# Sixteen up-projection groups of a two-layer encoder trunk computed with seven products in place of eight

## The chip, the cores and the metric

The kernel runs on one NeuronCore of one Trainium2 chip. The metric is device microseconds of one execution. The five engines have a queue each and are named as the profile names them: PE (TensorE, matrix products; PEld are its weight loads), DVE (VectorE), ACT (ScalarE), POOL (GpSimd) and SP (SyncE, which here issues the loads). Engines wait for one another by semaphores. Matrix results are accumulated in PSUM, eight banks of 128 partitions x 512 fp32 numbers; everything else lives in SBUF.

## The reference: what is computed

256 tokens of width 2048 in fp32 go through two layers, and each layer ends in a gated feed-forward part. Only that part is touched here:

```python
def conv_ffn(x, w_up, conv_w, conv_b, w_down):
    u = x @ w_up                                  # 256 x 2048 by 2048 x 11264
    up = jnp.pad(u, ((0, 0), (1, 1), (0, 0)))
    u = c[0] * up[:, :-2] + c[1] * up[:, 1:-1] + c[2] * up[:, 2:] + conv_b
    gate, val = jnp.split(u, 2, axis=-1)          # 5632 each
    return (jax.nn.silu(gate) * val) @ w_down     # 5632 x 2048

x = x + conv_ffn(rms_norm(x, norm_ffn[layer]), w_up[layer], conv_w[layer], conv_b[layer], w_down[layer])
```

Layer 0 has pooling and attention ahead of it, layer 1 an mLSTM; both of these end in an output projection with a residual add.

## The kernel before, in words

All products are made in fp32r from two parts. A weight chunk w (128x1024 fp32) is split by ACT into a rounded high part (L89) and by DVE into the remainder, the low part (L90); both go into a tile hl. Activations have a high and a low part too (xx, L266 and L269). A product is then three matmuls: high x high, high x low, low x high.

`Stream` holds the list of all weight chunks in the order in which they are used. `next()` hands out the next split chunk and keeps loads five chunks and splits two chunks ahead in the order of the program; raw chunks rotate through six buffers (pool wraw), split ones through four (wsplit). So a cast of a new chunk waits until PE has finished the chunk that used the buffer, and a load until DVE has split the chunk in its buffer.

PE's order is the order of the program text (manual_schedule); DVE's, ACT's, SP's and POOL's queues are ordered by a scheduler, which at each moment takes what its own time line says is ready. Each queue is then worked off strictly in order. `Weave` (wv) places side tasks among the groups: a task is a generator that yields a delay in estimated microseconds.

A feed-forward layer (ffn_layer) has 44 tiles f of 128 gate and 128 value columns, in chunks of FCH = 4, 8, 8, 8, 8, 8 tiles. An up group (up, stat_group, L203) takes four weight chunks; for each of 16 K tiles PE makes two matmuls of 512 columns and two of 256, with the weights stationary and the tokens moving, into two PSUM banks pairs of the pool mm (two buffers). Then gather (ACT copy L366, DVE add L367) joins the parts, L890 multiplies by the norm's scale R, L894 to L897 do the convolution, L900 to L903 the gate and the split of the result into gt. After the up groups of chunk c come the four down groups of chunk c-1 (down): activations stationary, weights moving 512 columns at a time; L376 adds the result to the residual x.

The norm ahead of a layer (class Norm) is applied late. squares and block run after each quarter of the residual: ACT's sums of squares, PE transposes (xt, L254), the parts xx. finish then makes the scale: nsum (L282), rv_n (L208), POOL's power, four short DVE steps re_n (L212 to L215), the diagonal dg (L294), PE's product with ones (npr, L203) and its copy R (L299). PE executes npr inside the fourth weight chunk of the layer's first up group.

The PSUM pool ps (four single banks) serves transposes and small products.

Of the kernel before, what the change touches and what calls it, by code (L numbers as in the profile page):

```python
# [9 lines left out]
F32 = mybir.dt.float32  # L10
F32R = mybir.dt.float32r
AF = mybir.ActivationFunctionType
ALU = mybir.AluOpType
# [3 lines left out]
P = 128  # L17
D = 2048
S = 256
KT = D // P  # L20
# [11 lines left out]
FT = DFF // P  # L32
FCH = [4, 8, 8, 8, 8, 8]
CH = 8
# [7 lines left out]
NB = D // 512  # L42
# [22 lines left out]
class Stream:  # L65


    def __init__(self, nc, wpool, spool, srcs, load_ahead, split_ahead):
        self.nc, self.wpool, self.spool, self.srcs = nc, wpool, spool, srcs
        self.la, self.sa = load_ahead, split_ahead  # L70
        self.w, self.hl = {}, {}
        self.n_load = self.n_split = self.at = 0

    def load(self, pieces=1):
        i = self.n_load
        width = self.srcs[i].shape[-1]
        n = width // pieces
        w = self.wpool.tile([P, CH * P], F32, tag="w", name=f"w{i}")
        for c in range(0, width, n):
            self.nc.sync.dma_start(w[:, c : c + n], self.srcs[i][:, c : c + n])  # L80
        self.w[i] = w, n, width
        self.n_load += 1

    def split(self, then=None):
        i = self.n_split
        w, n, width = self.w.pop(i)
        hl = self.spool.tile([P, 2, CH * P], F32R, tag="hl", name=f"hl{i}")
        for c in range(0, width, n):
            (self.nc.vector.tensor_copy if i + c == 0 else self.nc.scalar.copy)(hl[:, 0, c : c + n], w[:, c : c + n])  # L89
            self.nc.vector.tensor_sub(hl[:, 1, c : c + n], w[:, c : c + n], hl[:, 0, c : c + n].bitcast(F32))  # L90
            then and then(c // n)
        self.hl[i] = hl
        self.n_split += 1
# [63 lines left out]
def trunk(ctx: ExitStack, tc: tile.TileContext, gx, xT, xn, call, catt, cml, weights, out):  # L157
    nc = tc.nc
# [7 lines left out]
    actp = pool("act", 1)  # L166
# [16 lines left out]
    first = ExitStack()  # L183
# [179 lines left out]
    def gather(tp, ps, name):  # L363

        tb = tp.tile([P, 2, S], F32, tag="tb", name=f"tb_{name}")
        a.copy(tb, ps[:, :, 1, :])  # L366
        v.tensor_add(tb, ps[:, :, 0, :], tb)  # L367
        return tb

    def bc(ap, n):  # L370
        return ap.unsqueeze(1).to_broadcast([ap.shape[0], n, ap.shape[1]])

    def residual(ps, b, eng=None):
        for t in range(2):
            xs = x[:, t, b * 512 : b * 512 + 512]
            v.tensor_add(xs, xs, ps[:, t])  # L376
# [495 lines left out]
    def ffn_layer(layer, norm, nxt):  # L872
        with ExitStack() as es:
            def lp(name, bufs):
                return es.enter_context(tc.tile_pool(name=name, bufs=bufs, reuse_waits="tile"))

            tp = lp(f"ff{layer}", 2)

            def cw(tl, j):
# [6 lines left out]
            def up(f, gt, i):  # L886
                ps = stat_group(xx, list(range(KT)), f"up{layer}_{f}")
                wv.until(lambda: norm.R is not None)
                u = gather(tp, ps, f"up{layer}_{f}")
                v.tensor_mul(u, u, bc(norm.R, 2))  # L890
# [8 lines left out]
                s_ = tp.tile([P, S], F32, tag="silu", name=f"s{layer}_{f}")  # L899
                a.activation(s_, y[:, 0, :], AF.Silu)  # L900
                v.tensor_mul(s_, s_, y[:, 1, :])
                a.copy(gt[:, i, 0, :], s_)
                v.tensor_sub(gt[:, i, 1, :], s_, gt[:, i, 0, :].bitcast(F32))  # L903

            def down_end(gt, b, kts):
# [27 lines left out]
            def down(c, gt, last):  # L933
                kts = list(range(FCH[c]))
                for b in range(NB):
                    if last and nxt is None and b == NB - 1:
                        down_end(gt, b, kts)
                        break
                    ps = mmp.tile([P, 2, 512], F32, tag="mm", name=f"dn{layer}_{c}_{b}")
                    mov_part(ps, lambda k: gt[:, k], kts, True, True)  # L940
                    residual(ps, b)
                    if last and nxt is None:
                        nc.sync.dma_start(out[:, :, b * 512 : b * 512 + 512], x[:, :, b * 512 : b * 512 + 512])
                    elif last:
                        nxt.add(b)

            wv.add(norm.finish(), 4.0)
            f, gts = 0, []
            for c, n in enumerate(FCH):
                gt = actp.tile([P, 8, 2, S], F32R, tag=f"B{c % 2}", name=f"g{layer}_{c}")  # L950
                gts.append(gt)
                for i in range(n):
                    up(f, gt, i)
                    f += 1
                if c:
                    down(c - 1, gts[c - 1], False)
            down(len(FCH) - 1, gts[-1], True)

    norms = [Norm(0), None]
    norms[1] = Norm(1)  # L960
# [64 lines left out]
    return np.concatenate(out)  # L1025


def _ffn_order():

    seq, u, d = [], 0, 0  # L1030
    for c, n in enumerate(FCH):
        seq += [("u", u + i) for i in range(4 * n)]
        u += 4 * n
        if c:
            m = FCH[c - 1] // 4 * 8
            seq += [("d", d + i) for i in range(m)]
            d += m
    m = FCH[-1] // 4 * 8
    seq += [("d", d + i) for i in range(m)]
    return seq  # L1040


# [98 lines left out]
```

## Time and profile before

| | us |
|---|---|
| time, three runs | 2205.48, 2205.55, 2205.71; median 2205.55 |
| profiled execution, span from first to last instruction | 2203.1 |
| PE busy | 2197.9 (100%) |
| DVE busy | 1525.5 (69%) |
| ACT busy | 1169.0 (53%) |
| matmuls of the 88 up groups | 984.2 |
| matmuls of the down groups | 471.3 |
| feed-forward layers, from the stages | 256 to 990 and 1468 to 2203 |

The table's busy times are from the page's first and fifth parts. The span is what the profiled execution has of its own; the runs' times also hold what lies around it, 2.45 us against the median. In rows of groups, the columns are line, engine, operation, output <- inputs, shapes and count, then busy time, the mean of one in nanoseconds, and the idle time of the engine just before them with what ended it. Rows of the timeline and of the chain start with the start time and the length.

### The profile page before, as it was taken

How to read it: one execution, taken by the hardware profiler on the slowest of the kernel's cores; microseconds unless marked ns; L12 is line 12 of the kernel's file. 1: busy time of each engine (PE TensorE's matmuls, PEld its weight loads, DVE VectorE, ACT ScalarE, POOL GpSimd, SP SyncE). 2: the span in 40 equal slices, each digit the busy share in tenths (PEclk: the TensorE clock that was granted, in tenths of full speed). 3: DMA queues.
4: the chain of work that ended last, by engine and by line, in shares of the span. 5: the costliest groups of instructions: out<-in, count | busy, mean ns of one | idle time of the engine just before them, and what ended most of it. 6: DMA issues, size and time to landing. Idle time of an engine off the chain costs nothing.

```text
span 2203.1 us, 30458 instructions
## 1 busy us (share of the span) xinstructions
PE 2197.9 (100%) x11616; PEld 1883.7 (86%) x11616; DVE 1525.5 (69%) x2172; ACT 1169.0 (53%) x1664; POOL 28.1 (1%) x40
## 2 busy tenths in 40 slices
PE   9999999999999999999999999999999999999999
PEld 8888888888888888889888888888888888888887
DVE  7686677776776767666767676667777677676764
ACT  7665555554554545456555454555555455454542
POOL 0020000000000000000000000000000000000000
PEclk9999999999999999999999999999999999999999
DMA  9555556556565666656565555556555656555664
GB/s 323 179 164 170 175 191 187 190 189 198 184 194 188 192 191 191 196 171 205 162 202 177 185 181 171 186 177 191 186 191 189 197 185 193 189 191 191 192 191 144
DMA packets 118036, 415.71 MB, mean 189 GB/s; under 512 B 13082, under 2 KB 15426, under 8 KB 117890
## 3 DMA queue, kind: packets, MB, share of 16 engines
q1 hardware_dynamic: 114656, 409.76, 58.2%
q10 hardware_dynamic: 3074, 3.75, 0.6%
q8 instruction: 91, 1.49, 0.3%
q14 instruction: 55, 0.45, 0.1%
q0 software_dynamic: 160, 0.26, 0.0%
HBM read 411.58 MB, written 2.14 MB: 188 GB/s over the span
## 4 chain that ended last, share of the span: by engine, by line
PE 100%; DVE 0%; issue 0%
PE up L203 45%; PE dn L203 21%; PE op L203 8%; PE mv L203 4%; PE mq L203 4%; PE mk L203 4%; PE mo L203 4%; PE qproj L203 3%; PE pool L203 1%; PE kproj L203 1%; PE vproj L203 1%; PE qk L203 1%; PE av L203 1%; PE end L203 0%; PE xt L254 0%; PE sc L203 0%
## 5 line engine op out<-in xcount | busy, mean ns | idle before, releaser
L90 DVE TENSOR_TENSOR hl<-w,hl 128x1024 fp32r<-128x1024 f32 (+2 forms) x772 | 939.1, 1218 | 466.6 <-ACT hl L89 464.8
L89 ACT CAST hl<-w 128x1024 fp32r<-128x1024 f32 (+1 forms) x771 | 806.9, 1047 | 677.3 <-PE dn L203 242.1
L203 PE MATMUL up<-xx,hl 128*128 128x512 f32 (+1 forms) x5632 | 984.2, 337 | 0.0
L203 PEld LDWEIGHTS up<-xx,hl 128*128 128x128 f32 x5632 | 857.9, 188 | 125.9
L203 PE MATMUL dn<-hl,g 128*128 128x512 f32 x2064 | 471.3, 389 | 0.0
L203 PEld LDWEIGHTS dn<-hl,g 128*128 128x128 f32 x2064 | 386.2, 188 | 79.5
L366 ACT COPY tb_up<-up 128x512 f32<-128x512 f32 x88 | 51.7, 587 | 154.0 <-PE up L203 154.0
L367 DVE TENSOR_TENSOR tb_up<-up,tb_up 128x512 f32<-128x512 f32 x88 | 60.8, 691 | 97.0 <-ACT tb_up L366 97.0
L894 ACT ACTIVATE y<-tb_up,cst 128x256 f32<-128x256 f32 x176 | 96.4, 595 | 47.0 <-DVE tb_up L890 47.0
L203 PE MATMUL mk<-xx,hl 128*128 128x512 f32 (+1 forms) x512 | 92.2, 337 | 0.0
L203 PE MATMUL mq<-xx,hl 128*128 128x512 f32 (+1 forms) x512 | 92.1, 337 | 0.0
L203 PE MATMUL mv<-hl,xx 128*128 128x512 f32 (+2 forms) x480 | 91.7, 350 | 0.0
L203 PE MATMUL op<-hl,cat 128*128 128x512 f32 x384 | 91.6, 393 | 0.0
L203 PE MATMUL mo<-hl,xx 128*128 128x512 f32 x384 | 90.4, 391 | 0.0
L203 PE MATMUL op<-hl,mcat 128*128 128x512 f32 x384 | 89.5, 392 | 0.0
L203 PEld LDWEIGHTS mq<-xx,hl 128*128 128x128 f32 x512 | 79.2, 188 | 11.6
L203 PEld LDWEIGHTS mk<-xx,hl 128*128 128x128 f32 x512 | 79.0, 188 | 11.4
L203 PEld LDWEIGHTS mv<-hl,xx 128*128 128x128 f32 x480 | 78.3, 189 | 11.2
L203 PEld LDWEIGHTS op<-hl,mcat 128*128 128x128 f32 x384 | 71.5, 188 | 14.6
L203 PEld LDWEIGHTS mo<-hl,xx 128*128 128x128 f32 x384 | 71.0, 188 | 14.2
L203 PEld LDWEIGHTS op<-hl,cat 128*128 128x128 f32 x384 | 70.9, 188 | 14.1
L895 DVE SCALAR_TENSOR_TENSOR y<-tb_up,cst,y 128x255 f32<-128x255 f32 x176 | 76.8, 478 | 0.0
(209 smaller groups left out, 1270.4 us busy)
## 6 DMA issues: line engine op xcount, KB each, us to landing
w<-in_up SPq DMA_DIRECT2D x352, 512.0 KB, 3.6
w<-in_dn SPq DMA_DIRECT2D x176, 512.0 KB, 4.1
w<-in_m_in SPq DMA_DIRECT2D x124, 512.0 KB, 4.1
w<-in_a_in SPq DMA_DIRECT2D x46, 512.0 KB, 4.4
w<-in_a_out SPq DMA_DIRECT2D x32, 512.0 KB, 3.4
w<-in_m_out SPq DMA_DIRECT2D x32, 512.0 KB, 3.5
w<-in_m_g SPq DMA_DIRECT2D x5, 432.0 KB, 3.4
x<-in_xn SPq DMA_DIRECT2D x4, 512.0 KB, 9.5
```

Of the source, the lines that this page charges most:

```text
L89: (self.nc.vector.tensor_copy if i + c == 0 else self.nc.scalar.copy)(hl[:, 0, c : c + n], w[:, c : c + n])
L90: self.nc.vector.tensor_sub(hl[:, 1, c : c + n], w[:, c : c + n], hl[:, 0, c : c + n].bitcast(F32))
L203: pe.matmul(out_, lhsT, rhs, start=start, stop=stop, skip_group_check=True)
L366: a.copy(tb, ps[:, :, 1, :])
L367: v.tensor_add(tb, ps[:, :, 0, :], tb)
L894: a.activation(y[:, j, :], u[:, j, :], AF.Identity, scale=cw(tl, 1), bias=cw(tl, 3))
L895: v.scalar_tensor_tensor(y[:, j, 1:S], u[:, j, 0 : S - 1], cw(tl, 0), y[:, j, 1:S], ALU.mult, ALU.add)
```

## The change

For four of the eight tiles of chunks 2 and 4, in both layers, the four up groups are replaced by one "unit" (quads). The 256 tokens are two row tiles, the K tiles are taken in eight pairs, and the weights of the four tiles form two halves of 512 columns: a 2x2 by 2x2 block product for each K pair. It is made with seven block products instead of eight, Winograd's form: four in phase one (banks p1, p5, p6, p4), three in phase two (p5 and p6 again, p1 again). The activations are now stationary, so the result has tokens in partitions: ACT and DVE drain the banks into c11, c12, c21, c22 with the norm's scale on the way, PE transposes them back (finish), and the convolution follows as before (tail).

The seven products need sums. Sums of weights are made by DVE in the raw chunk before the split: one 128x512 add for a "sum" chunk, two for a "chain" chunk. A unit has 16 chunks in phase one (eight sum, eight chain) and 12 in phase two (eight sum, four plain), 28 where 16 stood. Sums of activations (sums, eight per half: one add of 128x2048, five of 128x512, then four casts and four subtractions) go to sx once per layer, as a side task.

The product chunks are spread between other groups (_ffn_plan): a unit's chunks lie one by one between the chunks of the up and down groups of the two chunks ahead, and down groups are now placed between up groups instead of behind them. Loads run seven and splits three chunks ahead, with one more raw and one more split buffer in the feed-forward layers. The gate is computed in place in y. The product, its plan and the two places that the prediction speaks of:

```diff
     def split(self, then=None):
         i = self.n_split
-        w, n, width = self.w.pop(i)
-        hl = self.spool.tile([P, 2, CH * P], F32R, tag="hl", name=f"hl{i}")
+        w, n, width, kind = self.w.pop(i)
+        hl = self.home(i, False).tile([P, 2, CH * P], F32R, tag="hl", name=f"hl{i}")
+        l, r = w[:, 0:512], w[:, 512:1024]
+        if kind == "sum":
+            self.nc.vector.tensor_add(r, r, l)
+            self.sum = r
+        if kind == "chain":
+            self.nc.vector.tensor_add(l, l, self.sum)
+            self.nc.vector.tensor_add(r, r, l)
...
+            def sums():
+                vv = actp.tile([P, 2, KT // 2, S], F32, tag="B1", name=f"v{layer}")
+                for h in range(2):
+                    ks = slice(8 * h, 8 * h + 8)
+                    v.tensor_add(vv[:, 0], norm.xx[:, ks, 0, :].bitcast(F32), norm.xx[:, ks, 1, :].bitcast(F32))
+                    yield 5.0
...
+                    v.tensor_sub(s1, a21, a22)
+                    v.tensor_add(s3, a11, a21)
+                    yield 3.0
+                    v.scalar_tensor_tensor(s2, s1, -1.0, a11, ALU.mult, ALU.subtract)
+                    v.tensor_sub(s4, s3, a12)
+                    v.tensor_sub(s4, s4, a22)
+                    yield 4.0
+                    for j in range(4):
+                        hi, lo = (sx[:, j, 4 * h : 4 * h + 4, i, :] for i in range(2))
+                        a.copy(hi, raw[:, j])
+                        v.tensor_sub(lo, raw[:, j], hi.bitcast(F32))
+                        yield 2.0
+            def product(bank, act, w, c, first, last):
+                (xh, xl), (wh, wl) = act, (w[:, j, c : c + 512] for j in range(2))
+                mm(bank, xh, wh, first, False)
+                mm(bank, xh, wl, False, False)
+                mm(bank, xl, wh, False, last)
+                wv.tick(0.68)
...
+                for p in range(m):
+                    ends = p == 0, p == m - 1
+                    hl = st.next()
...
+                    product(b1, block_of(2 * p, 0), hl, 0, *ends)
+                    product(b5, sum_of(0, p), hl, 512, *ends)
+                    yield
+                    hl = st.next()
...
+                    product(b6, sum_of(1, p), hl, 0, *ends)
+                    product(b4, block_of(2 * p + 1, 1), hl, 512, *ends)
+                    if p == m - 1:
+                        c12, c21, c22 = part(12), part(21), part(22)
+                        a.activation(c12, b1, AF.Copy, scale=n0)
+                        a.activation(c21, b1, AF.Copy, scale=r1)
+                        a.activation(c22, b5, AF.Copy, scale=r1)
+                        v.scalar_tensor_tensor(c12, b6, n0, c12, ALU.mult, ALU.add)
+                    yield
+                for p in range(m):
+                    hl = st.next()
+                    product(b5, sum_of(3, p), hl, 0, False, p == m - 1)
+                    product(b6, sum_of(2, p), hl, 512, False, p == m - 1)
...
+                    if p % 2:
+                        hl = st.next()
+                        for n in range(2):
+                            product(b1, block_of(2 * (p - 1 + n) + 1, 0), hl, n * 512, False, p - 1 + n == m - 1)
...
+            def finish(top, bottom, fs, gt, i0, name):
+                for n, f in enumerate(fs):
+                    tr = psp.tile([P, 2, S], F32, tag="ps", name=f"tr{layer}_{f}")
+                    for j in range(2):
+                        for t, src in enumerate((top, bottom)):
+                            c = (2 * j + n) * P
+                            pe.transpose(tr[:, j, t * P : t * P + P], src[:, c : c + P], ident)
+                    u = tp.tile([P, 2, S], F32, tag="tb", name=f"tb_{layer}_{f}")
+                    a.copy(u, tr)
+                    tail(u, f, gt, i0 + n)
+                    yield 2.5
...
             wv.add(norm.finish(), 4.0)
+            sx = xsp.tile([P, 4, KT // 2, 2, P], F32R, tag="sx", name=f"sx{layer}")
+            n0 = xsp.tile([P, 1], F32, tag="n0", name=f"n0_{layer}")
+            def sums_ready():
+                yield from wv.wait(lambda: norm.R is not None)
+                v.tensor_scalar_mul(n0, norm.rcol[:, 0:1], -1.0)
+                yield from sums()
+            wv.add(sums_ready(), 8.0)
+            st.la, st.sa, st.more = 7, 3, (lp(f"fw{layer}", 1), lp(f"fh{layer}", 1), st.at + len(_ffn_plan()))
...
+UNITS = {2: (1, 3), 4: (3, 5)}
+def _ffn_plan():
...
+    for c, (c0, c1) in UNITS.items():
+        lo, hi = begin[c0] + 2, begin[c1] - 7
+        one, two = 2 * m, m + m // 2
+        step = (hi - lo - 3) / (one + two)
+        for k in range(one + two):
+            here[int(lo + k * step + (3 if k >= one else 0))].append(("s", c, 0))
```

More of the change, by code (lines that the diff above doesn't have):

```diff
@@ L877, in ffn_layer @@
             tp = lp(f"ff{layer}", 2)
+            xsp = cp1 = lp(f"fs{layer}", 1)
             def cw(tl, j):
@@ L884, in xx, with tail @@
                 return norm.at(k)
[L886 to L890, printed above, removed]
+            def tail(u, f, gt, i):
                 y = tp.tile([P, 2, S], F32, tag="y", name=f"y{layer}_{f}")
@@ L903, in up @@
                 v.tensor_sub(gt[:, i, 1, :], s_, gt[:, i, 0, :].bitcast(F32))
+            def up(f, gt, i):
+                ps = mmp.tile([P, 2, 2, S], F32, tag="mm", name=f"up{layer}_{f}")
+                for q in range(KT // 4):
+                    stat_part(ps, xx, list(range(4 * q, 4 * q + 4)), q == 0, q == KT // 4 - 1)
+                    if q < KT // 4 - 1:
+                        yield
+                wv.until(lambda: norm.R is not None)
+                u = gather(tp, ps, f"up{layer}_{f}")
+                v.tensor_mul(u, u, bc(norm.R, 2))
+                tail(u, f, gt, i)
@@ L931, in down_end, with down @@
                     nc.sync.dma_start(out[:, t, b * 512 + c0 : b * 512 + c1], xs)
-            def down(c, gt, last):
+            def down(c, gt, b):
                 kts = list(range(FCH[c]))
[L935 to L945, printed above, removed]
@@ L947, in ffn_layer @@
-            wv.add(norm.finish(), 4.0)
[L948 to L957, printed above, removed]
+                last = c == len(FCH) - 1
+                if last and nxt is None and b == NB - 1:
+                    down_end(gt, b, kts)
+                    return
@@ new lines, in down @@
+                ps = mmp.tile([P, 2, 512], F32, tag="mm", name=f"dn{layer}_{c}_{b}")
+                for k in range(0, len(kts), 2):
+                    mov_part(ps, lambda k: gt[:, k], kts[k : k + 2], k == 0, k == len(kts) - 2)
+                    if k < len(kts) - 2:
+                        yield
+                residual(ps, b)
+                if last and nxt is None:
+                    nc.sync.dma_start(out[:, :, b * 512 : b * 512 + 512], x[:, :, b * 512 : b * 512 + 512])
+                elif last:
+                    nxt.add(b)
@@ new lines, in ffn_layer @@
+            gts, run = {}, {}
+            for step in _ffn_plan():
+                kind, c = step[:2]
+                if kind != "d" and c not in gts:
+                    gts[c] = actp.tile([P, 8, 2, S], F32R, tag=f"B{c % 2}", name=f"g{layer}_{c}")
+                key = step[:3]
+                if key not in run:
+                    f0 = sum(FCH[:c])
+                    run[key] = (up(f0 + step[2], gts[c], step[2]) if kind == "n" else
+                                down(c, gts[c], step[2]) if kind == "d" else
+                                quads([f0 + 4 + j for j in range(4)], gts[c], 4, f"{layer}_{c}"))
+                next(run[key], None)
@@ L959, in trunk @@
+            for e in run.values():
+                assert next(e, None) is None
+            st.la, st.sa, st.more = 5, 2, None
     norms = [Norm(0), None]
@@ new lines, in _ffn_order @@
+def _ffn_order(up, dn, one, two, three):
+    pos, seq = {}, []
+    m = KT // 2
+    d0 = [sum(FCH[:c]) // 2 * NB for c in range(len(FCH))]
+    for step in _ffn_plan():
+        kind, c, i = step
+        n = pos.get(step, 0)
+        pos[step] = n + 1
+        if kind == "n":
+            seq.append(up[(sum(FCH[:c]) + i) * 4 + n])
+        elif kind == "d":
+            seq.append(dn[d0[c] + i * (FCH[c] // 2) + n])
+        else:
+            u = list(UNITS).index(c)
+            if n < 2 * m:
+                seq.append((("sum", "chain")[n % 2], one[u, n // 2, n % 2]))
+            else:
+                n -= 2 * m
+                seq.append(three[u, n // 3] if n % 3 == 2 else ("sum", two[u, n // 3 * 2 + n % 3]))
@@ L1129, in ffn @@
     def ffn(l):
-        u, d = chunks(f"up{l}"), chunks(f"dn{l}")
-        return [(u if w == "u" else d)[j] for w, j in _ffn_order()]
+        return _ffn_order(chunks(f"up{l}"), chunks(f"dn{l}"), *(t[f"q{j}{l}"] for j in range(3)))
     n = 3 * (MD + 32)
```

94 lines of the change are left out of this document (79 added, 15 removed).

## The prediction

> **What bounds the kernel now.** First the page's first and fourth parts, the busy shares and the chain that ended last.
>
> ```profile
> PE 2197.9 (100%) x11616; PEld 1883.7 (86%) x11616; DVE 1525.5 (69%) x2172; ACT 1169.0 (53%) x1664; POOL 28.1 (1%) x40
> PE 100%; DVE 0%; issue 0%
> PE up L203 45%; PE dn L203 21%; PE op L203 8%; PE mv L203 4%; PE mq L203 4%; PE mk L203 4%; PE mo L203 4%; PE qproj L203 3%; PE pool L203 1%; PE kproj L203 1%; PE vproj L203 1%; PE qk L203 1%; PE av L203 1%; PE end L203 0%; PE xt L254 0%; PE sc L203 0%
> ```
>
> TensorE (PE) never rests: only fewer or shorter matmuls shorten the kernel, and any stop of PE lengthens it one for one. Then the stages of the feed-forward layer (up groups, then down groups), and the waits.
>
> ```profile
> core 0: us, PE busy (x) PEld busy (x) DVE busy (x) ACT busy (x) POOL busy (x), PEclk, DMA share, GB/s
> 413.00:502.20 89.20, 89.20 (x514) 77.84 (x513) 64.58 (x90) 48.97 (x67) 0.00 (x0) 1.00 0.59 189
> 502.20:545.70 43.50, 43.50 (x193) 36.00 (x193) 26.64 (x30) 19.07 (x21) 0.00 (x0) 1.00 0.61 194
> ...
> DVE hl L90 <- ACT hl L89: 464.8, 427, 2.6
> ACT hl L89 <- PE dn L203: 242.1, 157, 1.8
> ACT hl L89 <- PE up L203: 209.4, 182, 1.7
> ```
>
> VectorE (DVE) is busy 72% of an up stage and 61% of a down stage. What idles is cover: DVE waits for ScalarE (ACT), which waits for PE to give a split buffer back. The weight splits run ahead of PE and PE sets their pace.
>
> **What the change takes from PE.** The unit prices are rows of the chain in order of time (start, length, what); the last row is from the groups of instructions.
>
> ```profile
> 413.01 89.16 PE up L203 x512
> 502.18 43.53 PE dn L203 x192
> 259.62 0.44 PE xt L254 x4
> ...
> L203 PE MATMUL op<-hl,cat 128*128 128x512 f32 x384 | 91.6, 393 | 0.0
> ```
>
> Sixteen up groups go (four tiles in each of two chunks, two layers), 64 matmuls each: 1024 x 89.16/512 = 178.3 us. In their place stand four units of 8 K pairs x 7 products x 3 matmuls = 168, together 672. Each streams 512 columns against a 128x128 activation block, as the down groups do: 672 x 43.53/192 = 152.4 us. The four finished quarters are turned back by 16 blocks of four 128x128 transposes; xt blocks are the same form: 16 x 0.44 = 7.0 us. PE's own work changes by -178.3 + 152.4 + 7.0 = **-18.9 us**. If the products ran at the slowest group rate (91.6 us for 384, the op<-hl,cat group), they would be 8 us dearer; that group has waits and other matmuls between, so I take the down rate.
>
> ```profile
> L90 DVE TENSOR_TENSOR hl<-w,hl 128x1024 fp32r<-128x1024 f32 x762 | 930.7, 1223 | 463.3 <-ACT hl L89 461.5
> L890 DVE TENSOR_TENSOR tb_up<-tb_up,R 128x512 f32<-128x512 f32 x88 | 60.9, 692 | 3.0
> L89 ACT CAST hl<-w 128x1024 fp32r<-128x1024 f32 x762 | 800.1, 1050 | 674.3 <-PE dn L203 239.7 <-PE up L203 209.4 <-PE op L203 68.8
> w<-in_up SPq DMA_DIRECT2D x352, 512.0 KB, 3.6
> ...
> GB/s 323 179 164 170 175 191 187 190 189 198 184 194 188 192 191 191 196 171 205 162 202 177 185 181 171 186 177 191 186 191 189 197 185 193 189 191 191 192 191 144
> ...
> 260.04 1.22 DVE L90 TENSOR_TENSOR hl<-w,hl 128x1024 fp32r<-128x1024 f32 x1
> 261.18 0.15 DVE L213 TENSOR_TENSOR re_n<-re_n,rv_n 128x2 f32<-128x2 f32 x1
> 281.16 0.69 DVE L890 TENSOR_TENSOR tb_up<-tb_up,R 128x512 f32<-128x512 f32 x1
> 281.77 1.22 DVE L90 TENSOR_TENSOR hl<-w,hl 128x1024 fp32r<-128x1024 f32 x1
> ```
>
> Above are group rows (mean ns of one behind the busy time), the load's row (KB, us to landing), the page's GB/s by slice, and four rows of the timeline (start, length): start to start a 1024-wide DVE operation takes 1.14 us (260.04 to 261.18) and a 512-wide one 0.61 (281.16 to 281.77), 0.08 less than alone.
>
> **What it adds off PE, inside the units.** A product chunk holds as many weights as any other but feeds 6 matmuls (1.36 us of PE) instead of 12 to 16 (2.7 to 2.8). So each unit has 28 chunks where 16 stood: 12 more loads, casts (1.05) and splits (1.22), and 32 adds of 128x512 that form weight sums (0.69). That is 12 x 1.22 + 32 x 0.69 = 37 us more DVE a unit. Does it fit? In the changed order, from one up group's gather to the next in phase one, PE has four up chunks, two down chunks and three product chunks: 11.1 + 5.4 + 4.1 = 20.7 us. DVE has nine splits, four sum adds, gather, scaling, two residual adds and a tail (2.3, four shifted adds and two short operations): 9 x 1.14 + 8 x 0.61 + 2.3 = 17.4 us, 84%. The fullest stretch, where a unit's four tiles are finished at once, has 11 splits, nine 512-wide operations and three to four tails, 26 us, against 26.5 of PE (98%). At every gather PE has 8 to 13 us of split chunks ahead (five buffers instead of four). I therefore cost this at nothing; with that lead gone, each missing microsecond of DVE would be PE's. ACT's casts add 12 x 1.05 = 13 us a unit to a 55% engine, nothing. The 48 loads (25 MB, all behind SP's queue, two raw tiles of which are now issued early into a new buffer) meet a queue whose share is 0.60; the densest stretch asks for 6.3 chunks in 14.6 us, 225 GB/s, which the page's first slice (323 GB/s) exceeds. A sum add that waits for its load (3.6 us to landing) holds the DVE queue behind it; it costs up to 1.2 us of the slack, not of PE. The banks drained between the phases (three ACT copies, one DVE operation) have five other chunks, 13.7 us, before the next product; the transposes come 10 us after the last add they need. Both at nothing.
>
> **What it adds at the start of each feed-forward layer.** Here the cover is gone. The activation sums (32 DVE operations a layer) are ready as soon as the out-projection's last residual is added, and the instruction order puts them among the norm's end. In the kernel before that stretch reads:
>
> ```profile
> 256.19 1.28 DVE L376 TENSOR_TENSOR x<-x,op 128x512 f32<-128x512 f32 x2 [0.41 <-PE op L203]
> 257.39 1.22 DVE L90 TENSOR_TENSOR hl<-w,hl 128x1024 fp32r<-128x1024 f32 x1
> ...
> 261.25 0.48 DVE L269 SCALAR_TENSOR_TENSOR xx<-xt,gcol,xx 128x256 fp32r<-128x256 f32 x1
> 261.65 0.16 DVE L214 TENSOR_SCALAR re_n<-re_n 128x2 f32<-128x2 f32 x1
> 261.75 0.48 DVE L269 SCALAR_TENSOR_TENSOR xx<-xt,gcol,xx 128x256 fp32r<-128x256 f32 x1
> ...
> 262.68 0.47 DVE L294 TENSOR_SCALAR dg<-cst,re_n 128x128 f32<-128x128 f32 x2
> ...
> 266.11 0.43 PE npr L203 x2
> 1468.05 1.28 DVE L376 TENSOR_TENSOR x<-x,op 128x512 f32<-128x512 f32 x2 [0.41 <-PE op L203]
> 1477.98 0.43 PE npr L203 x2
> ```
>
> The norm's scale (nsum, rv_n, re_n, then the diagonal dg) is finished at 263.1, and PE's npr matmul, which takes dg and stands in PE's fixed order inside the first up group's fourth chunk, runs at 266.1 without waiting: 3 us to spare. In the changed order npr stands at the same place, but dg comes much later in DVE's queue; each of the four re_n steps, dependent on the one before, has let ready sums pass. From the residual to dg the changed queue holds, in both layers alike:
>
> ```
> residual x2, v 128x2048, split, nsum, v x2, split, xx, rv_n, xx, v x2, sx x2, split, xx, re_n, xx, v, sx,
> split, re_n, v 128x2048, sx, re_n, v x2, re_n, v x2, dg x2
> ```
>
> Start to start: two residuals 1.20; two 2048-wide adds, by the step of 0.53 from 512 to 1024, 1.14 + 2 x 0.53 = 2.20 each, 4.4; four splits 4.56; nine 512-wide v and four sx 13 x 0.61 = 7.9; four xx 1.6 (261.25 to 261.65); six tiny ones 0.6 (261.65 to 261.75); dg 0.47. Sum 20.8 us, from 256.19 to 277.0, and npr at 277.1: a **PE stop of 11.0 us**, and in the other layer from 1468.05 to 1488.9 against 1477.98, 11.0 again. Ends: without the six tiny ones and 0.08 of each of the other 27 (2.8 us less) 8.2; every operation at its full duration 13.2. Everything of PE queues behind npr, the first gather too (it needs R); the splits of the next four chunks stand before dg, so after the stop PE is fed. Two stops: +22.0 us.
>
> PE then starts from rest. The only start from rest in this trace is the kernel's own:
>
> ```profile
> 1.24 4.62 PE wps L227 x10
> 5.86 22.16 PE kproj L203 x96
> ...
> 1.20:2.40 1.20, 1.18 (x3) 1.00 0.53 93
> ```
>
> The same form (npr, 128x256, x2) takes 0.43 in full run, so ten would take 2.15: 2.5 us were lost, though the granted clock reads 1.00 there (last row: stretch, its length, PE busy, clock, DMA share, GB/s). Per stop I take 2.5, the row nearest to a start from rest; the low end is 0 (a short stop need not cool it), the high end 2.9, with what kproj's 96 lost after it (22.16 less 96 x 0.227). Two: **+5.0 us**. [...]
>
> **Sum.** 2203.1 - 18.9 + 22.0 + 5.0 = 2211.2 us of span. The profiled span is 2.45 below the median of the runs (2205.55); what lies around it stays, so **2213.6 us**, 0.4% slower.
>
> **The rivals.**
> (a) The sums are hidden after all: faster. For it: DVE idles in every stage. Against: the queue above. It decides below 18.9/2 = 9.5 us for stop and slow restart together; with none at all the time is 2203.1 - 18.9 + 2.45 = 2186.6. Chance 0.10.
> (b) The stop, but no slow restart: 2208.6, no measurable change. For it: PE's clock column never leaves 1.00. With stops a little shorter also 2204. Chance 0.20.
> (c) The stops, and DVE also falls behind in phase one. A unit's phase one has 8 pairs of product chunks, each with 4.3 other chunks, 14.6 us of PE against 12.9 of DVE (13.6 us slack together) and 8.2 of lead; its 16 chunk adds would have to wait 1.6 us each for loads (25.6 us) to use that up, 3.8 us of PE a unit, 15 in all: 2229. Chance 0.12.
> (d) The forecast, 2208 to 2219: 0.58.
>
> **Numbers.** About 0.2% (4.4 us) is what a measurement can tell from no change: 2201.1 to 2210.0. Slower: all of (c) and (d) and a little of (b), 0.72; same: most of (b), 0.18; faster 0.10. The range that leaves out (a), the far part of (c) and the low part of (b) is 2205 to 2223; (d)'s own ends are 2203.1 - 18.9 + 16.4 + 2 x 2.5 + 2.45 = 2208 with the shortest stops and 2203.1 - 18.9 + 26.4 + 5.8 + 2.45 = 2219.
>
> **What would show it.** Right: two places of PE idle of about 11 us, released by DVE's dg, near 266 and near 1460 to 1480, DVE busy throughout, matmuls after them at half pace for some microseconds; product groups at 0.227 us a matmul; transposes 0.44 a block; no other PE idle. Wrong: dg early, PE's busy share still 100% (a); or PE idle before product chunks, released by ACT or DVE splits (c).

## The result: 0.95% slower

| | before | after |
|---|---|---|
| time, median | 2205.5 us | 2226.4 us (2223.9, 2224.3, 2228.5, 2228.9) |
| ratio, 95% interval | | 1.0095 (1.0081 to 1.0109) |
| profiled execution, time and span | 2205.5, 2203.1 | 2224.3, 2222.0 |

2213.6 was forecast, with 2223 as the upper end. The direction was right, the size was not: 20.9 us slower instead of 8.1. Two single executions in the experiments, one with the adds kept in place (2764 us) and one with the products in pairs (3361 us), ran at a granted clock of 0.75 and 0.60, and no reading rests on them.

### The profile page after: what moved, and what is told of

The parts are those of the page before. It is cut to its first block, busy times and chain, and to the rows that moved or that the text cites. A ratio compares the mean times of both kernels' runs of the same rounds, so it can differ in the third digit from the quotient of the medians.

```text
span 2222.0 us, 30399 instructions
## 1 busy us (share of the span) xinstructions
PE 2193.0 (99%) x11328; PEld 1864.8 (84%) x11328; DVE 1668.8 (75%) x2378; ACT 1228.3 (55%) x1744; POOL 28.1 (1%) x40
## 4 chain that ended last, share of the span: by engine, by line
PE 85%; DVE 6%; DMA 6%; issue 2%; ACT 0%; DVEq 0%; ACTq 0%
PE up L219 27%; PE dn L219 20%; PE op L219 8%; DMA w<-in_q 6%; PE p L219 5%; PE mv L219 4%; PE mq L219 4%; PE mk L219 4%; PE mo L219 4%; DVE hl L106 3%; PE qproj L219 3%; PE kproj L219 1%; PE pool L219 1%; PE vproj L219 1%; PE qk L219 1%
## 5 line engine op out<-in xcount | busy, mean ns | idle before, releaser
L106 DVE TENSOR_TENSOR hl<-w,hl 128x1024 fp32r<-128x1024 f32 (+1 forms) x820 | 992.3, 1217 | 295.8 <-ACT hl L105 291.7
L105 ACT CAST hl<-w 128x1024 fp32r<-128x1024 f32 (+1 forms) x819 | 851.7, 1047 | 570.6 <-PE up L219 185.5
L219 PE MATMUL up<-xx,hl 128*128 128x512 f32 (+1 forms) x4608 | 829.7, 338 | 1.9 <-DVE hl L106 1.9
L219 PEld LDWEIGHTS up<-xx,hl 128*128 128x128 f32 x4608 | 719.5, 189 | 114.6 <-DVE hl L106 4.8
L219 PE MATMUL dn<-hl,g 128*128 128x512 f32 x2064 | 485.0, 391 | 0.6 <-DVE hl L106 0.6
L908 ACT ACTIVATE y<-tb_up,cst 128x256 f32<-128x256 f32 x144 | 78.8, 595 | 84.6 <-DVE tb_up L927 83.5
L219 PE MATMUL p<-hl,sx 128*128 128x512 f32 x384 | 104.2, 393 | 0.0
L99 DVE TENSOR_TENSOR w<-w 128x512 f32<-128x512 f32 x64 | 44.3, 692 | 76.4 <-DMA w<-in_q 76.2
L382 ACT COPY tb_up<-up 128x512 f32<-128x512 f32 x72 | 42.2, 586 | 102.6 <-PE up L219 100.3
```

What stands on the lines that cost most here:

```text
L99: self.nc.vector.tensor_add(r, r, l)
L219: pe.matmul(out_, lhsT, rhs, start=start, stop=stop, skip_group_check=True)
```

## The profile after

First the page's busy shares and its chain by engine, then the waits of the kernel after (engine, what it waited for, microseconds in total, how often, the longest).

```profile
PE 2193.0 (99%) x11328; PEld 1864.8 (84%) x11328; DVE 1668.8 (75%) x2378; ACT 1228.3 (55%) x1744; POOL 28.1 (1%) x40
PE 85%; DVE 6%; DMA 6%; issue 2%; ACT 0%; DVEq 0%; ACTq 0%
```

```profile
PE npr L219 <- DVE n L1085: 21.3, 2, 10.7
PE up L219 <- DVE hl L106: 1.9, 5, 0.8
...
PE dn L219 <- DVE hl L106: 0.6, 2, 0.4
DVE hl L106 <- ACT hl L105: 291.7, 270, 2.6
DVE w L99 <- DMA w<-in_q: 76.2, 57, 3.7
...
DVE w L102 <- DMA w<-in_q: 35.9, 23, 3.5
SPq L89 <- DVE hl L106: 1480.4, 637, 13.9
```

PE was the whole chain before; now 12% of it runs through DVE and loads. Three things are new. PE waits twice for the norm (npr), 10.7 us each. PE waits seven times, 2.5 us together, for splits (hl) inside the feed-forward layers, where the prediction allowed no wait at all. And DVE waits 80 times, 112 us together, for the load of a weight chunk at the first add on it (L99, L102). The last line closes a circle: SP's loads wait for DVE's splits to give a raw buffer back (in the kernel before too, 1386.6 us in 545 waits; the adds in between are what is new).

The stop in layer 0, from the timeline (start, length, and in brackets the idle time before and its releaser):

```profile
255.98 1.28 DVE L392 TENSOR_TENSOR x<-x,op 128x512 f32<-128x512 f32 x2 [0.41 <-PE op L219]
257.18 2.28 DVE L935 TENSOR_TENSOR v<-xx 128x2048 f32<-128x2048 f32 x1
...
270.59 2.29 DVE L935 TENSOR_TENSOR v<-xx 128x2048 f32<-128x2048 f32 x1
...
275.94 0.48 DVE L310 TENSOR_SCALAR dg<-cst,re_n 128x128 f32<-128x128 f32 x2
...
276.56 1.19 PE L219 MATMUL npr<-dg,cst 128*128 128x256 f32 x2 [10.66 <-DVE n L1085]
```

dg ends 20.4 us behind the residual's start (275.94 + 0.48 - 255.98; 20.8 was forecast), because both 2048-wide sums and their followers stand ahead of it. Then the stretches just behind the stop (length, PE busy and matmuls, granted clock, DMA share, GB/s):

```profile
276.50:279.00 2.50, 2.44 (x7) 0.50 0.00 0
279.00:281.60 2.60, 2.60 (x12) 0.67 0.00 0
281.60:284.20 2.60, 2.60 (x17) 1.00 0.03 6
```

PE starts at half clock (0.50; the two npr take 1.19 us, and 0.60 in the first experiment below, where the clock is 1.00) and has all of it back 4.2 us after npr begins. In layer 1 npr begins at 1496.84 and the half clock lasts longer, 5.9 us:

```profile
1498.60:1501.20 2.60, 2.60 (x9) 0.50 0.00 0
1501.20:1503.80 2.60, 2.60 (x13) 0.71 0.00 0
```

By the granted clock of 0.50 half of these 4.2 and 5.9 us is lost: 2.1 and 2.9 us, 5.0 together.

## The experiments

All medians below are set beside the kernel before in the same job (2205.5 to 2205.6).

### The sums behind the norm

The first activation add gets a factor of one that is computed from R, so DVE cannot do it before the norm is finished.

```diff
+            one = xsp.tile([P, 1], F32, tag="one", name=f"one{layer}")
                 v.tensor_scalar_mul(n0, norm.rcol[:, 0:1], -1.0)
+                v.tensor_scalar(one, norm.R[:, 0:1], 0.0, 1.0, ALU.mult, ALU.add)
...
-                    v.tensor_add(vv[:, 0], norm.xx[:, ks, 0, :].bitcast(F32), norm.xx[:, ks, 1, :].bitcast(F32))
+                    v.scalar_tensor_tensor(vv[:, 0], norm.xx[:, ks, 0, :].bitcast(F32), one,
+                                           norm.xx[:, ks, 1, :].bitcast(F32), ALU.mult, ALU.add)
```

> The activation sums are given a factor of one that is computed from R, so that DVE does them after the norm's dg and R instead of ahead of them. Theory (the two stops of 10.7 us stand in DVE's queue order, and TensorE's half pace behind them is their consequence): both stops and both slow restarts go, 21.3 + 4.7 = 26 us, so 2200.4 us; the granted clock is 1.00 throughout. Rival 1 (the half pace behind the stop has another cause): only 21.3 us go, 2205. Rival 2 (the sums are now late and hold up the splits of the weights, so the wait moves): TensorE waits for hl by 5 us or more in the 40 us after the norm, 2210 to 2216.

Measured: 2195.2 us (2194.7 to 2196.8), ratio to before 0.9954 (0.9940 to 0.9967): faster than both kernels. Its timeline:

```profile
262.86 0.47 DVE L310 TENSOR_SCALAR dg<-cst,re_n 128x128 f32<-128x128 f32 x2
...
266.12 0.60 PE L219 MATMUL npr<-dg,cst 128*128 128x256 f32 x2
```

and the only wait of PE that it has in the feed-forward layers:

```profile
PE dn L219 <- DVE g L917: 3.1, 2, 1.5
```

dg is 13 us earlier and npr does not wait. The gain, 31.2 us, is 5 more than the two stops and restarts (26), and the waits for hl are gone too, while two new ones for a gate g have come. So the theory held for the stops, but this edit changed something else as well. The later runs show what it was.

### The weight adds kept at their place in the program

```diff
-            self.nc.vector.tensor_add(r, r, l)
+            self.pin(self.nc.vector.tensor_add(r, r, l))          # pin: tc.keep_in_program_order
             self.sum = r
...
-            self.nc.vector.tensor_add(l, l, self.sum)
+            self.pin(self.nc.vector.tensor_add(l, l, self.sum))
```

> The first weight sum of each product chunk is kept at its place in the program, so that on DVE it comes 5 to 15 instructions later, just ahead of its own chunk's split; the stops stay. Theory (DVE is blocked in its queue by sums that wait for a load which the order took as landed): DVE's waits for loads at the three add lines fall from 112 us to under 20, TensorE's 7 waits for hl with them, and the time falls by 4 to 9 us to 2217 to 2222, with less spread between executions than the 5 us of the kernel after. Rival (DVE has room enough, and these waits cost TensorE nothing but 2.5 us): 2224 to 2226.

> Both edits. Theory: the gains add, 26 + 4 to 9 us, so 2191 to 2196 us, which is faster than before (2205.5). Rival (the second edit gives nothing once DVE is not late any more): as with the first edit alone, about 2200.

Measured: 2294.3 us (ratio 1.0407, 1.0393 to 1.0421) for this edit alone and 2279.7 (1.0335, 1.0321 to 1.0349) with the sums behind the norm. Both expectations failed by far. The first add's group in the first of them (busy time, mean; then idle time in front), and PE's waits there:

```profile
L100 DVE TENSOR_TENSOR w<-w 128x512 f32<-128x512 f32 x64 | 43.8, 685 | 0.0
```

```profile
PE p L220 <- ACT hl L106: 35.1, 16, 6.3
PE p L220 <- DVE hl L107: 15.5, 18, 1.3
```

The adds no longer wait for any load, as expected. But now they stand on average 2.8 DVE operations ahead of their chunk's split where the kernel after has 13.6, and the cast of the chunk must wait for them: PE waits 50.6 us in front of the products, and the mean granted clock falls to 0.987. The edit cured the symptom and made the split late. It says nothing for or against the waiting adds as the cause; the next two do.

### Without the weight adds

```diff
-        if kind == "sum":
-            self.nc.vector.tensor_add(r, r, l)
-            self.sum = r
-        if kind == "chain":
-            self.nc.vector.tensor_add(l, l, self.sum)
-            self.nc.vector.tensor_add(r, r, l)
```

> The kernel after without the additions on the raw weights; stops and restarts stay. Theory (the 4.5 us of waits for hl inside the units, and the 5 us between its executions, come from additions that stand in DVE's queue and wait for a load): 2219 to 2222, all executions within 1.5 us of each other. Rival (both come from something else, such as the splits being late since the stop): 2224 to 2229 with the same spread.

> As the kernel with the sums after the norm, and without the additions on the raw weights (64 of the first line, 48 and 48 of the other two, 110 us of DVE): the chunks are split and multiplied as they land, so that their products are not those of the scheme. Theory (with the stops gone the additions cost only the two waits for g, 3.1 us, which came from a full DVE): 2195.2 - 3.1 = 2192, and DVE's waits for loads at the splits stay small. Rival 1 (they also cause the 5.7 us that are left above the bare sum of 2186.6): 2186 to 2188. Rival 2 (they cost nothing at all): 2195.

Both kernels leave the weight sums out, so they do not compute the layer; they are only for timing. (The adds are 64, 32 and 32 operations, 88.4 us of DVE; the figures of the second text were too high.) Measured: from the kernel after 2219.8 (2218.1 to 2220.0), 6.6 us less than with the adds; with the sums behind the norm 2189.05 (2188.8 to 2189.3). In the first the only wait of PE in the feed-forward layers is the norm's:

```profile
PE npr L213 <- DVE n L1079: 21.3, 2, 10.7
```

So the adds cost the kernel after 6.6 us, though the waits for hl that the page names are only 2.5 (PE's delays in these places, from start to start of the matmuls, come to 4.5, as much as lies between the two profiled executions). The edit takes away the adds' own 88 us of DVE together with their waits, and does not tell the two apart. And 2189.05 lies between the two expectations of the second run: the bare work of the change is 2.4 us above the forecast's 2186.6. But the two runs differ by 30.75 us, where stops and restarts explain 26. Of the rest, 4.0 us are found by setting the matmuls of the two traces side by side, one to one. Those of the dn groups whose weights came from one of the five split buffers took 233.4 ns from start to start instead of 226.9; those of the products from this buffer took 4.1 ns more, and the dn matmuls of the chunk right behind it 1.8 ns more. In the program's memory plan that buffer begins at byte 218336 in the kernel after, an odd multiple of 32, and at 218368, a multiple of 64, in the kernels with the tile `one`, which takes 32 bytes ahead of it.

### The split buffer moved by 32 bytes

The kernel after with one unused tile, and (with a cheaper layout of the work, next section) the reverse.

```diff
             n0 = xsp.tile([P, 1], F32, tag="n0", name=f"n0_{layer}")
+            xsp.tile([P, 1], F32, tag="gap", name=f"gap{layer}")
```

> The kernel after, with one more tile of 32 bytes a partition in the pool of the activation sums, which nobody uses: the same instructions in the same order, but the fifth split buffer (one chunk in five of the up and down groups and the products) lies at 218368 instead of 218336 bytes, that is, on a multiple of 64. Theory (TensorE reads its streamed operand slower from the odd multiple of 32: 233.4 ns a matmul for the 192 matmuls of dn in a layer that come from this buffer, where the others have 227 to 228): the dn matmuls go to 227 all alike and the time falls by 2 x 2.1 = 4.2 us to 2222.2. Rival (the 5 ns come from what else is different about these chunks): 2226.4, the 192 matmuls as slow as before.

> The kernel with the sums after the norm and the first down-projection one group later, with 32 bytes more in the pool of the activation sums, so that the fifth split buffer lies at 218400, an odd multiple of 32; the same instructions in the same order. Theory of the address: 4.2 us slower, 2193.2, with the 192 matmuls of dn in a layer from this buffer at 233 ns. Rival: 2189.0.

Measured: 2221.4 (2217.4 to 2224.7), 5.0 us less than the kernel after, though the ranges of the two overlap a little; and 2194.3 (2194.2 to 2194.7) against 2189.04 of the same kernel without the gap, 5.3 us more. Both ways, with no instruction changed. The dn groups of the second pair (busy time and mean behind the bar), then the same 24 matmuls, half of them from this buffer, in the timeline; each time first without and then with the gap:

```profile
L219 PE MATMUL dn<-hl,g 128*128 128x512 f32 x2064 | 481.2, 390 | 0.0
```

```profile
L219 PE MATMUL dn<-hl,g 128*128 128x512 f32 x2064 | 484.4, 391 | 0.0
```

```profile
450.40 5.60 PE L219 MATMUL dn<-hl,g 128*128 128x512 f32 x24
```

```profile
450.78 5.72 PE L219 MATMUL dn<-hl,g 128*128 128x512 f32 x24
```

Matmul by matmul the second pair loses 5.2 us, 3.2 in the dn groups, 0.7 in the products and 1.2 in the up groups; the first loses 3.9, the same in dn groups and products and nothing in the up groups, and what else lies between its medians is not placed. The gap moves the extra raw buffer and the units' results by the same 32 bytes, but the loss sits in every fifth chunk, that of the split buffer, and the one behind it, and the transposes of the results are no slower. The theory of the address holds, with 3.9 and 5.2 us where 4.2 was expected. Why the up groups lose time in one pair alone is open.

### The first down group one up group later, and products in pairs

Both start from the kernel with the sums behind the norm. The first gives chunk 0's last gate one more up group of time; the second takes two product chunks in a row.

```diff
             fill = sum(([*fill[per * b : per * b + per], ("d", c - 1, b)] for b in range(NB)), [])
+            if c == 1:
+                k = fill.index(("d", c - 1, 0))
+                fill.insert(k, fill.pop(k + 1))
```

```diff
-            here[int(lo + k * step + (3 if k >= one else 0))].append(("s", c, 0))
+            here[int(lo + (k - k % 2) * step + (3 if k >= one else 0))].append(("s", c, 0))
```

> As the kernel with the sums after the norm, with the first down-projection of chunk 0 one up group later, so that the last gate of chunk 0 has 5.7 us more. Theory (the two waits of 1.5 us for g, and little else, go): 3.1 us less, 2192. Rival (DVE's lateness passes to the next thing that TensorE needs): 2195.

> As the kernel with the sums after the norm, with the product chunks taken in pairs, one behind the other, so that TensorE changes between products and groups half as often. Theory (each change costs some 0.05 us, 5.7 us for the 112 chunks): 2.8 us less, 2192.4. Rival 1 (the 5.7 us lie in the products themselves, 231 ns a matmul where the groups have 227): 2195.2. Rival 2 (two chunks' additions in a row hold up DVE): 2197 or more, with new waits for hl.

> The kernel with the sums after the norm and the first down-projection one group later, with the product chunks in pairs. Theory (the 2.4 us that are left above 2186.6 come with the change between a product chunk and a group, 1.381 us for six matmuls where 1.360 were counted): half of it goes, 2187.9. Rival 1 (they lie in the products themselves): 2189.0. Rival 2 (the 3.2 us that the pairs gave to the kernel with the sums after the norm are a gain of their own): 2185.8.

Measured: later 2189.04 (2188.9 to 2189.2), in pairs 2191.9, both 2191.9. Where the 3.2 us that the pairs alone won come from, no trace shows. The move gave 6.1 us instead of 3.1. Most of the reason is in the kernel without it: from start to start of the matmuls each of the two waits for g, both 1.53 us of idle time, held PE back 1.7 us, and the second cost more than that. Its timeline at both places, and the stretches behind the second (length, PE busy and matmuls, granted clock, DMA share, GB/s):

```profile
336.51 1.20 PE L219 MATMUL dn<-hl,g 128*128 128x512 f32 x4 [1.53 <-DVE g L917]
337.55 2.94 PE L219 MATMUL up<-xx,hl 128*128 128x512 f32 x16
...
1542.37 1.68 PE L219 MATMUL dn<-hl,g 128*128 128x512 f32 x4 [1.53 <-DVE g L917]
1543.85 4.08 PE L219 MATMUL up<-xx,hl 128*128 128x512 f32 x16
```

```profile
1542.00:1544.00 2.00, 1.63 (x5) 0.72 0.83 268
1544.00:1546.00 2.00, 2.00 (x8) 0.50 0.29 117
1546.00:1548.00 2.00, 2.00 (x13) 0.93 0.00 0
```

Behind the second the granted clock fell to a half for 3.4 us (0.28, 0.50 and 0.07 of 2 us are missing, 1.7 us in all), behind the first it did not. That makes 5.1 of the 6.1 us. So a wait of 1.5 us had a stretch at half clock behind it once and not the other time; no trace shows what sets the two apart. From 200 us on, every stretch at half clock ahead of PE's last matmul in ten of the traces lasts 3.41, 6.83, 10.24 or 13.65 us, one to four times 3.41: 3.41 here, 10.24 and 13.65 in the kernel after, and 6.83 once with the weight adds kept in place.

The account of the kernel with the sums behind the norm closes with this: 26.3 for stops and restarts, 5.0 for the address and 6.6 for the waits of the adds, less these 6.1, make 31.8 against 31.2 measured.

With the move, the waits that the adds make for loads are fewer, and PE is busy throughout (waits of the kernel with the move, then its page):

```profile
DVE w L99 <- DMA w<-in_q: 54.2, 43, 4.1
...
DVE w L102 <- DMA w<-in_q: 17.5, 12, 2.0
```

```profile
PE 2181.6 (100%) x11328; PEld 1861.6 (85%) x11328; DVE 1668.3 (76%) x2380; ACT 1231.1 (56%) x1744; POOL 28.2 (1%) x40
```

The same time as without any weight add: with the stops gone and this cover, 88 us of adds and 72 us of waiting for loads on DVE cost nothing. The pairs together with the move made a new wait, since the units' ends came closer to their transposes:

```profile
PE tr L1027 <- DVE c L1006: 3.2, 4, 0.8
```

### The pairs, with the transposes later

```diff
-                            wv.add(finish(c12, c22, fs[2:], gt, i0 + 2, name), 3.0)
-                            wv.add(finish(c11, c21, fs[:2], gt, i0, name), 5.0)
+                            wv.add(finish(c12, c22, fs[2:], gt, i0 + 2, name), 5.5)
+                            wv.add(finish(c11, c21, fs[:2], gt, i0, name), 7.5)
```

> The kernel in pairs and one group later, with the transposes at a unit's end 2.5 us later by the plan's clock, so that they no longer wait for the last scalar additions (3.2 us in four waits). Theory (this wait took the 0.9 us back that the pairs gave): 2188.1. Rival (the wait goes to the gates that need these transposes): 2191 to 2192.

Measured: 2187.55 us (2187.5 to 2188.0), ratio to before 0.9918 (0.9905 to 0.9932), the best version: 18.0 us faster than the kernel before. The wait for c is gone. 1.5 us below the unpaired kernel, 1.0 of it in the product chunks: from start to start they take 1.371 us each instead of 1.381, where six matmuls at 227 ns make 1.362. With half as many changes between product chunks and groups, half of the excess is gone.

### The stops with PE kept busy

44 matmuls that nobody reads fill the stop ahead of npr, first in the kernel after. Then the same in a kernel that has the move and the aligned buffer, next to that kernel without them.

```diff
+            for k in range(44):
+                mm(pr, self.xx[:, 0, 0, 0:P], self.xx[:, 2 * (k % 4), :, :].rearrange("p a b -> p (a b)"), True, True)
             mm(pr[:, 0:S], ones, dg.rearrange("p a b -> p (a b)"), True, True)
```

> 44 matmuls of 128x512, whose result nobody reads, go ahead of the norm's own matmul, 10.0 us of work inside the stop of 10.7 us. Theory (the half pace behind the stop comes from the stop's idleness): the granted clock stays 1.00, both stops are as long as before, and the time falls by the two slow restarts, 2.0 + 2.7 = 4.7 us, to 2221.7. Rival (the half pace, or the lost time behind the stop, has another cause, such as late splits): no change, 2226.4.

> The kernel after with the first down-projection one group later and the fifth split buffer on a multiple of 64 bytes; the activation sums stand ahead of the norm's last steps again, so that both stops are back and all else is as in the fast kernel of 2189.0. Theory (stop and slow restart are a fixed price: 10.8 us of waiting, 0.4 us for the norm's own matmul at half pace and 2.1 us for the groups behind it, each twice): 26.6 us more, 2215.6, within 1 us from execution to execution. Rival (DVE is late behind the stops, so that the additions hold up TensorE again in the units): 2219 to 2224, with waits for hl and a spread of several us.

> The same with 44 matmuls of 128x512 in each stop, whose result nobody reads. Theory (the slow restart comes from the idle time alone): the granted clock is 1.00 throughout and only the two waits of 10.8 us are left, 2189.0 + 21.7 = 2210.7. Rival (the restart is slow for another cause): 2215.6 as without these matmuls.

Measured: 2219.1 (2216.8 to 2221.5), 7.3 us less than the kernel after; 2221.0 (2220.2 to 2222.2) and, with the matmuls, 2216.0 (2214.6 to 2217.8). The mean granted clock is 1.000 with the matmuls and 0.994 or 0.995 without. So the slow restart comes from idleness. Its price is less sharp than the 5.0 us between these two kernels, because with the matmuls PE also waits less for hl, 2.2 us instead of 4.7 (0.7 instead of 2.5 in the first pair). The waits of the kernel with the matmuls:

```profile
PE up L219 <- DVE hl L106: 1.7, 3, 0.8
...
PE dn L219 <- DVE hl L106: 0.5, 1, 0.5
```

Read from the granted clock, the two restarts cost 5.0 us in the kernel after and 4.3 in the kernel here without the matmuls (3.1 and 5.5 us at half clock). The kernel with the stops back and without the matmuls lies on its rival's side: the waits for hl are back too, although the down group is later and the buffer aligned.

```profile
PE npr L219 <- DVE n L1086: 21.3, 2, 10.7
PE up L219 <- DVE hl L106: 2.8, 5, 0.9
PE dn L219 <- DVE hl L106: 1.9, 2, 1.3
```

One such wait in that kernel's timeline, with the load that it starts from (SPq rows are issues):

```profile
398.59 0.33 SPq L89 DMA_DIRECT2D w<-in_q  x1
...
403.15 0.69 DVE L102 TENSOR_TENSOR w<-w,w 128x512 f32<-128x512 f32 x1 [3.45 <-DMA w<-in_q]
403.76 0.68 DVE L383 TENSOR_TENSOR tb_up<-up,tb_up 128x512 f32<-128x512 f32 x1
404.36 0.68 DVE L103 TENSOR_TENSOR w<-w 128x512 f32<-128x512 f32 x1
404.96 1.22 DVE L106 TENSOR_TENSOR hl<-w,hl 128x1024 fp32r<-128x1024 f32 x1
...
406.23 5.38 PE L219 MATMUL up<-xx,hl 128*128 128x256 f32 x30 [0.94 <-DVE hl L106]
```

The add stands ahead of a split that PE needs at once. Its load was issued at 398.59 and landed 4.56 us later; DVE idled 3.45 us in front of it, and the split, whose cast had ended at 401.78, ended at 406.18. PE waited 0.94. Why this happens with the stops and not without them is not settled: the scheduler's DVE order differs between the two kernels (the adds stand 13.5 operations ahead of their split with the stops, 12.7 without), and the stops also leave DVE other work to catch up with. No run here separates the two.

## Why the prediction was wrong, point by point

| term | predicted, us | measured, us |
|---|---|---|
| PE's own work | -18.9 | -16.5 (2189.05 against 2205.5) |
| two stops | +22.0 | +21.3 (waits) |
| two slow restarts | +5.0 | +5.0 (2221.0 - 2216.0, and by the granted clock) |
| inside the units | 0 | +6.6 (2226.4 - 2219.8; 4.5 between the profiled executions) |
| place of the fifth split buffer | not named | +5.0 and +5.3 (3.9 and 5.2 by the matmuls) |

With +5.0 for the buffer the measured column adds up to +21.4; the kernel is 20.9 slower. The last two rows are needed together to pass 2223: without the buffer the column gives 2221.9.

**The stops** came as the queue had been counted: npr at 276.6 instead of 277.1, and a stop of 10.7 us instead of 11.0, in both layers alike, with DVE busy throughout. The activation sums are 20 DVE operations a layer and not 32, but the forecast goes by the queue, which lists the 15 that stand ahead of dg. Rival (a), hidden sums, is what the kernel with the sums behind the norm makes true.

**The slow restart** came at the size of the row it was taken from, the kernel's own start; rival (b) fell. That the two make just 5.0 is partly luck: a single restart cost between 1.6 and 3.1 us in the traces with stops (3.1 to 6.2 us at half clock). The granted clock of four traces gives 4.3 to 5.2 for the two.

**PE's own work** was 2.4 us too cheap. Start to start, the 112 chunks of six products take 1.381 us each, 154.7 where 152.4 stood; the transposes take 0.355 a block, 5.7 where 7.0 stood. That leaves 1.4. The prediction took the other groups as unchanged, but in the kernel of 2189.04 the 4608 matmuls that are left of the up groups take 174.57 ns from start to start where 174.29 stood, 1.3 us, and the down groups 0.5 us more in all, which covers it. The pairs gave 1.5 back, so the cost goes with the interleaving, which a price from unbroken down groups could not hold.

**The step that failed** is "I therefore cost this at nothing". It set DVE's work against PE's and found 84%, with 8 to 13 us of lead, and said that a sum add waiting for its load costs only slack. But DVE's queue is worked off in order (in the timeline above a split whose cast had ended at 401.78 begins at 404.96, behind an add that kept DVE idle for 3.45 us), and the loads of the product chunks took 4.2 us to land where 3.6 had been taken. DVE's free time stood in front of the adds (112 us), where nothing behind them could use it, and a load that an add waited for had itself waited for an earlier split. The timeline above shows one such wait reach PE; without the adds all of them are gone. What the adds cost hangs on what else DVE is late with. With the sums behind the norm it is 6.1 us (2195.2 against 2189.05), through the two waits for g, and nothing once the first down group stands one up group later. How the adds and the stops together make DVE late stays open. The adds that wait for loads are rival (c)'s mechanism, at 6.6 us instead of 15, and not where (c) had looked for it: PE waited in front of up and down groups, not of products.

**What was not named at all** is where the new buffers lie. The prediction costed the instructions of the fifth split buffer and took its matmuls at the price of the other four; no run here shows a reason for the slower ones other than the address.

Open is also why executions of the kernel after differ by up to 5 us (2223.9 to 2228.9). The restarts do not explain it, since the mean granted clock is 0.994 or 0.995 in all four. The kernels without weight adds, or where the adds make PE wait nowhere, stay within 2 us and mostly within 0.5.

## What to carry to other kernels

Work that DVE's in-order queue could take "when it is ready" was not free here, though DVE was busy for only 75% of the span: ask what stands behind it, above all a short dependent chain (here four steps on two columns) that another engine waits for, and, if it takes a load, how long the queue sits in front of it. A data dependence (a factor of one taken from the norm's result) moved the sums out of the way and, with 5 us from the moved buffer, turned +20.9 into -10.4 us; holding operations at a fixed place made them too late. When a pool is added, look at the start address of what TensorE streams: 32 bytes were worth 5.0 and 5.3 us here.

## What the runs showed of the hardware that was not expected

One split buffer, which TensorE streams as its moving operand (128x512, fp32r), made matmuls slower where it began at an odd multiple of 32 bytes (218336 and 218400) than where it began at 218368: in the kernel after 233.4 ns a matmul instead of 226.9 in the dn groups, and some 4 ns more in the products. For this one buffer in five that is 3.9 and 5.2 us of the kernel by the matmuls (5.0 and 5.3 by the medians), shown by moving it by 32 bytes in both directions.

Of two equal waits of 1.53 us in one execution one had a granted clock of 0.50 for 3.4 us behind it, the other 1.00.

The stretches at half clock lasted 3.41, 6.83, 10.24 and 13.65 us, one to four times 3.41. The stops of 10.7 us had stretches of 10.24 or 13.65, and between 3.1 and 6.2 us of PE's work behind them ran at half clock.
